# Stick-breaking attention in a fused decoder: one strict order for vector and scalar work, and weights split at fixed places of a turn

## The chip, the cores and the metric

The kernel runs on one core of a Trainium2 chip. Four engines matter here, and each takes its instructions in its own queue: TensorE (PE, matmuls; the loading of its stationary operand is listed as PEld), VectorE (DVE), ScalarE (ACT) and GpSimd (POOL). SyncE (SP) issues the transfers from memory. The metric is the device time of one execution, in microseconds (us).

## The reference, cut to what matters

A decoder trunk of two layers over 512 tokens of width 2048, in float32. The first layer is sparse attention; the second is stick-breaking attention with 16 query heads in four groups over four shared key/value heads, and a gate. The change touches the second layer only:

```python
q, gate = jnp.split(x @ w_in, [WIDTH_B], axis=-1)
z = jnp.einsum('bqngd,bsnd->bngqs', qg, k) * (HEAD_DIM ** -0.5)
log_om = jnp.where(strict, -jax.nn.softplus(z), 0.0)
suffix = lax.cumsum(log_om, axis=log_om.ndim - 1, reverse=True) - log_om
a = jnp.where(strict, jnp.exp(jax.nn.log_sigmoid(z) + suffix), 0.0)
o = jnp.einsum('bngqs,bsnd->bqngd', a, v)
return (o * jax.nn.silu(gate)) @ w_o
```

A token sees strictly earlier keys only; its weight for a key is a sigmoid times the product of what all keys between have left over, computed in log space.

## The kernel before

**Precision.** Each float32 product is made of three matmuls: every operand is split into a high part (a rounding copy on ScalarE) and a low part (a subtraction on VectorE), by `split` (line 131), and `mm3` (line 135) adds high by high, high by low and low by high in one PSUM bank.

**Two streams on TensorE.** TensorE's order is written out by hand. In the stage around the change it alternates between the gate projection and the attention of one group of four heads. The gate of a group is 64 *steps*: 16 blocks of weights by four banks, a step being one `mm3` into one bank (`gemm_w`, line 289; for group 0 `gate_first`, line 1214, which takes the blocks 8 to 15 first). A block of weights comes from the generator `items`: `next_raw` (line 179) issues its transfer, `split` makes the tiles wh and wl, of which there are three each.

**The attention** of a group (`Sticks`, line 1240) has ten units, pairs of a block of 128 queries and a block of 128 keys. The units with equal block numbers (0, 1, 5 and 8) lie on the diagonal and are masked. A unit passes through these methods:

- `logits`: three matmuls into a bank z; on the diagonal VectorE adds the mask. Unit 0 uses bank 7, the others banks 4 and 5 in turn.
- `soft` (abs, exp and ln on ScalarE) and `plus` (VectorE) make the softplus sp.
- `high` adds what earlier keys left (total) and makes sh on VectorE, and copies rows of z to t on ScalarE; `low` makes sl.
- `weights`: two matmuls with a triangular matrix add the running sum to z; ScalarE takes the exponential; VectorE subtracts z from t.
- `halves` splits the result a into high (ScalarE) and low (VectorE); `values`: three matmuls; `leave` copies a finished output.

`turn(s)` (line 1346) runs unit s's logits to `low`, unit s-1's `weights` and `halves`, and unit s-2's `values`, with gate steps in three gaps between.

**What sets the order on VectorE and ScalarE.** A planner orders what the program emits by a model of the time. Operations under `paced` (line 325) are recorded with `keep_in_program_order`; all others, the splits of the gate's weights above all, stand where the planner puts them. In the built program even paced operations of different kinds pass each other in places. Other splits lie in the deque `bg`: the next group's queries (`split_scaled`, line 1208), keys (`split_keys`) and the restoring of half of x's tiles (`restore`, line 1148). `pumped` (line 339) runs one of them every so many gate steps.

**Between groups** (lines 1398 to 1422) the two first logits of the next group come first, then four SiLUs of the gate's banks with a product each, then a table load for exp and ln (`log_exp`, line 1223), then `begin` for units 0 and 1. The SiLU's own table load is inserted by the compiler ahead of the first SiLU.

Of the kernel before, what the change touches and what calls it, by code (L numbers as in the profile page):

```python
# [77 lines left out]
def trunk_kernel(  # L78
# [17 lines left out]
    pe = nc.tensor  # L96
    pinned = [False]

    class Paced:


        def __init__(self, engine):
            self.engine_ = engine

        def __getattr__(self, name):
            method = getattr(self.engine_, name)
            if not callable(method):
                return method

            def call(*args, **kw):  # L110
                ins = method(*args, **kw)  # L111
# [96 lines left out]
    class Ahead:  # L208
# [13 lines left out]
        def __next__(self):  # L222
            self.prime()
            it = next(self.items, None)
            if it is not None:
                self.waiting.append(it)
            return self.waiting.popleft()

    def weight_parts():
        return tuple(top.tile([128, 512], F32R, name=n, tag=n, bufs=3) for n in ("wh", "wl"))  # L230

# [91 lines left out]
    bg = deque()  # L323

    def paced(fn, *args):
        was, pinned[0] = pinned[0], True
        fn(*args)
        pinned[0] = was

    def one():  # L330
        paced(bg.popleft())
# [270 lines left out]
    items = Ahead(all_items(), 2)  # L602
# [16 lines left out]
    late = slice(NSEL, T)  # L619
# [84 lines left out]
    banks = late_banks(range(4))  # L704
    gemm = gemm_w(items, late_plain, banks)
# [32 lines left out]
    banks = [bank(b, "v") for b in (4, 5, 6, 7)]  # L738
# [130 lines left out]
    for g in range(4):  # L869
        banks = mm_banks("g")  # L870
# [293 lines left out]
    def split_keys(g):  # L1164
        split(*K[g], Kf[:, g])
# [42 lines left out]
    def split_scaled(g, i):  # L1208
        qh, ql = (q.rearrange("p (h q) -> p h q", h=4) for q in Q[i])
        src = F[g][:, :, i * 128 : (i + 1) * 128]  # L1210
        act.activation(qh, src, AF.Copy, scale=HSCALE)
        dve.scalar_tensor_tensor(ql, src, HSCALE, qh.bitcast(F32), ALU.mult, ALU.subtract)

    def gate_first(banks):

        for kb in (*range(8, NK), *range(8)):
            wh, wl = next(items)
            for j, out in enumerate(banks):
                s = slice(j * 128, (j + 1) * 128)
                mm3(out, (wh[:, s], wl[:, s]), plain(kb), kb == 8, kb == 7)  # L1220
                yield

    def log_exp():
        tc.keep_in_program_order(act.preload_act_table_set("natural_log_exp_and_others"))

    def work():
        return px.tile([128, 512], F32, name="wk", tag="wk", bufs=6)

# [11 lines left out]
    class Sticks:  # L1240
# [101 lines left out]
        def begin(self, u):  # L1342
            for fn in (self.soft, self.plus, self.high, self.low):
                paced(fn, u)

        def turn(self, s, gemm, gaps):

            late = self.diagonal(s)
            if 1 < s < 10:
                paced(self.logits, s)  # L1350
                if late:
                    paced(self.low, s - 1)
                paced(self.soft, s)
                if not late:
                    paced(self.plus, s)
            steps(gemm, gaps[0])
            if s > 1:
                paced(self.values, s - 2)
            steps(gemm, gaps[1])
            if s < 11:  # L1360
                paced(self.weights, s - 1)
                if 1 < s < 10 and late:
                    paced(self.plus, s)
                paced(self.halves, s - 1)
                if 1 < s < 10:
                    paced(self.high, s)
                    if not self.diagonal(s + 1):
                        paced(self.low, s)
# [7 lines left out]
    QUERIES_DONE = {8: (1,), 9: (3,), 11: (0,)}, {5: (1,), 9: (3,), 11: (0,)}  # L1376

    log_exp()

    def after_combining(fn, *args):  # L1380
        with tc.issue_after(combined):
            fn(*args)

    bg.extend(lambda i=i: after_combining(split_scaled, 0, i) for i in (3, 1))
    banks = mm_banks("g")
    chunk = gate_first(banks)
    gemm = pumped(chunk)
    sticks = Sticks(0)
    for u, n in enumerate((9, 1)):
        steps(gemm, n)  # L1390
        paced(sticks.logits, u)
    for u in range(2):
        sticks.begin(u)
    bg.extend(lambda i=i: split_scaled(0, i) for i in (2, 0))
    steps(gemm, 8)
    gemm = pumped(chunk, 2)

    for g in range(4):
        if g:
            steps(gemm, 12)  # L1400
            bg.append(lambda g=g: split_scaled(g, 2))
        if 0 < g < 3:
            bg.append(lambda g=g: split_keys(g + 1))
        for s in range(1, 12):
            sticks.turn(s, gemm, (0 if s == 1 else 1, 1 if s > 1 else 0, 2 if s == 10 or not g and s % 2 else 3))
        run(gemm)
        drain()
        if g < 3:
            then = Sticks(g + 1)
            for u in range(2):  # L1410
                paced(then.logits, u)
        for h in range(4):
            sg = work()
            act.activation(sg, banks[h], AF.Silu)
            dve.tensor_tensor(F[g][:, h], F[g][:, h], sg, ALU.mult)
        if g < 3:
            sticks = then
            log_exp()
            for u in range(2):
                sticks.begin(u)  # L1420
# [60 lines left out]
```

## Time and profile before

| what | us |
|---|---|
| median of 3 runs (1878.97 to 1879.47) | 1879.23 |
| the profiled execution's own time | 1879.65 |
| its span, first to last instruction | 1877.9 |
| busy TensorE, VectorE, ScalarE | 1860.1, 1233.5, 938.0 |
| stick-breaking stage, from its first gate step to the first matmul of the output projection | 1233.96 to 1501.62 |

The profiled execution is the source of every duration below. In rows of the timeline the columns are the start in us from the start of the span, the length in us, engine, line, operation, output, inputs in the program's names, shapes, and in brackets the idle time before it with what ended it. `L111` is the helper that records every VectorE and ScalarE operation. Names: g are the gate's banks, z the logits, wh and wl the weight tiles, wk work tiles of the softplus and the weights, sh and sl its halves, c the tiles of keys, queries, values and of a, o the attention's output, f the stream. In rows by stretch the columns stand in the order PE, PEld, DVE, ACT, POOL (busy us, number of instructions), granted clock, DMA share, GB/s.

### The profile page before, as it was taken

The page shows a single profiled execution, that of the slowest core. Times are in us where ns is not written, and L with a number is a line of the kernel's source. Part 1 is how long each engine was busy: PE and PEld are TensorE (multiplying, and loading weights), DVE is VectorE, ACT ScalarE, POOL GpSimd, SP SyncE. Part 2 cuts the span into 40 slices and gives each one's busy share as a digit, 9 for nine tenths or more (in the row PEclk, how much of TensorE's full clock was granted, in tenths as well). Part 3 has the DMA queues.
Part 4 walks back from the last instruction along what each step waited for, and adds up shares of the span by engine and source line. Part 5 has one row for each costly group of instructions (what it writes and reads, how often), then busy time and mean ns, then how long its engine had stood idle before and what let it go on. Part 6 is the DMA issues. An engine that isn't in the chain of part 4 may idle for free.

```text
span 1877.9 us, 24827 instructions
## 1 busy us (share of the span) xinstructions
PE 1860.1 (99%) x9181; PEld 1573.8 (84%) x9181; DVE 1233.5 (66%) x2395; ACT 938.0 (50%) x1696; POOL 4.7 (0%) x20
## 2 busy tenths in 40 slices
PE   9999999999999999999999999999999999999998
PEld 8898888888888888888888999987777788888887
DVE  5668678566555455675367788887877745567534
ACT  3546333456554432474245444467778743347422
POOL 0000000000000000000000000000000000000000
PEclk9999999999999999999999999999999999999999
DMA  6442333322222532433343333322122253242333
GB/s 196 127 124 58 100 95 97 100 58 68 68 68 68 171 107 77 123 96 112 118 134 119 102 102 102 110 83 78 56 68 67 67 180 101 73 129 91 123 101 113
DMA packets 111178, 189.21 MB, mean 101 GB/s; under 512 B 8528, under 2 KB 29008, under 8 KB 111056
## 3 DMA queue, kind: packets, MB, share of 16 engines
q1 hardware_dynamic: 111056, 187.62, 32.5%
q8 instruction: 72, 1.18, 0.3%
q14 instruction: 50, 0.41, 0.1%
HBM read 179.21 MB, written 8.39 MB: 100 GB/s over the span
## 4 chain that ended last, share of the span: by engine, by line
PE 96%; DVE 2%; ACT 1%; issue 0%; DMA 0%; SPq 0%; DVEq 0%
PE g L136 12%; PE g L137 12%; PE g L138 12%; PE o L138 7%; PE o L137 7%; PE o L136 7%; PE m L136 4%; PE m L138 4%; PE m L137 4%; PE q L136 3%; PE q L138 3%; PE q L137 3%; PE k L137 2%; PE k L138 2%; PE k L136 2%; PE iq L138 1%
## 5 line engine op out<-in xcount | busy, mean ns | idle before, releaser
L111 ACT ACTIVATE wh<-raw 128x512 fp32r<-128x512 f32 (+3 forms) x685 | 397.7, 581 | 696.1 <-PE g L137 227.9
L111 DVE TENSOR_TENSOR wl<-raw,wh 128x512 fp32r<-128x512 f32 (+3 forms) x685 | 430.6, 629 | 453.3 <-ACT wh L111 434.7
L136 PE MATMUL g<-xh,wh 128*128 128x512 f32 x1024 | 403.9, 394 | 0.0
L138 PE MATMUL g<-xh,wl 128*128 128x512 f32 x1024 | 399.6, 390 | 0.0
L137 PE MATMUL g<-xl,wh 128*128 128x512 f32 x1024 | 399.5, 390 | 0.0
L138 PEld LDWEIGHTS g<-xh,wl 128*128 128x128 f32 x1024 | 192.2, 188 | 41.3
L137 PEld LDWEIGHTS g<-xl,wh 128*128 128x128 f32 x1024 | 192.5, 188 | 37.1
L136 PEld LDWEIGHTS g<-xh,wh 128*128 128x128 f32 x1024 | 192.4, 188 | 36.9 <-issue 0.3
L138 PE MATMUL o<-xh,wl 128*128 128x512 f32 x512 | 199.3, 389 | 0.0
L136 PE MATMUL o<-xh,wh 128*128 128x512 f32 x512 | 199.2, 389 | 0.0
L137 PE MATMUL o<-xl,wh 128*128 128x512 f32 x512 | 199.2, 389 | 0.0
L138 PEld LDWEIGHTS o<-xh,wl 128*128 128x128 f32 x512 | 96.1, 188 | 20.3 <-DVE wl L111 0.4
L137 PEld LDWEIGHTS o<-xl,wh 128*128 128x128 f32 x512 | 96.1, 188 | 20.1
L136 PEld LDWEIGHTS o<-xh,wh 128*128 128x128 f32 x512 | 96.1, 188 | 19.9
L136 PE MATMUL q<-xh,wh 128*128 128x512 f32 x256 | 99.6, 389 | 0.0
L137 PE MATMUL q<-xl,wh 128*128 128x512 f32 x256 | 99.6, 389 | 0.0
L138 PE MATMUL q<-xh,wl 128*128 128x512 f32 x256 | 99.6, 389 | 0.0
L111 ACT ACTIVATE sh<-st 128x512 fp32r<-128x512 f32 x80 | 49.7, 624 | 44.2 <-DVE st L111 44.2
L111 ACT ACTIVATE wk<-z 128x512 f32<-128x512 f32 x80 | 47.4, 593 | 43.1 <-PE z L1310 21.0
L111 DVE TENSOR_TENSOR sl<-st,sh 128x512 fp32r<-128x512 f32 x80 | 55.2, 690 | 13.9 <-ACT sh L111 13.9
L111 DVE TENSOR_TENSOR xl<-f,xh 128x512 fp32r<-128x512 f32 x80 | 54.3, 686 | 12.6 <-ACT f L111 12.3
L138 PEld LDWEIGHTS q<-xh,wl 128*128 128x128 f32 x256 | 48.0, 188 | 10.1
(287 smaller groups left out, 3319.0 us busy)
## 6 DMA issues: line engine op xcount, KB each, us to landing
raw<-w_in_a SPq DMA_DIRECT2D x95, 512.0 KB, 3.7
raw<-w_in_b SPq DMA_DIRECT2D x64, 512.0 KB, 3.7
raw<-w_ple_gate SPq DMA_DIRECT2D x52, 512.0 KB, 3.7
raw<-w_o_a SPq DMA_DIRECT2D x24, 512.0 KB, 3.7
raw<-w_o_b SPq DMA_DIRECT2D x24, 512.0 KB, 3.7
raw<-w_kv_b SPq DMA_DIRECT2D x16, 512.0 KB, 3.8
raw<-w_ple_gate SPq DMA_DIRECT2D x24, 256.0 KB, 2.9
f<-xT SPq DMA_DIRECT2D x4, 1024.0 KB, 6.3
```

What stands on the lines that cost most here:

```text
L111: ins = method(*args, **kw)
L136: pe.matmul(out, a[0], b[0], start=start, stop=False)
L137: pe.matmul(out, a[0], b[1], start=False, stop=False)
L138: pe.matmul(out, a[1], b[0], start=False, stop=stop)
```

## The change

All VectorE and ScalarE work of the stage is put in one order. A third state of the recorder (`pinned[0] == 2`, set by the new `strictly`) places each operation behind the one recorded before it on the same engine. The weight splits are under it too: `Fed` wraps `items` so that `push` emits the next block's splits and `next` only hands out what is there; `feed` pushes blocks until those that the next ten gate steps need are there. It is called inside a turn behind `plus` (one block at most, not in turns that begin on a diagonal unit), near the turn's end, and around the groups' starts. The splits in `bg` run at the ends of turns (`others`), one a turn, two in group 0. The SiLU table is loaded in turn 11 ahead of the last `leave`. The gate steps have new shares (`TURNS`): 17 instead of 18 ahead of group 0's first turn, 10 instead of 12 ahead of those of the later groups, a second step ahead of `values` in turns 5 and 8. `log_exp`, `begin`, `pumped` and `drain` are no longer used in this stage.

```diff
             def call(*args, **kw):
-                ins = method(*args, **kw)
-                if pinned[0]:
-                    tc.keep_in_program_order(ins)
+                if pinned[0] == 2 and self in newest:
+                    with tc.issue_after(newest[self].ins):
+                        ins = method(*args, **kw)
+                else:
+                    ins = method(*args, **kw)
+                    if pinned[0]:
+                        tc.keep_in_program_order(ins)
+                if pinned[0] == 2:
+                    newest[self] = ins
                 return ins
...
+        def push(self):
+            it = next(self.items, None)
+            if it is not None:
+                self.count += 1
+                self.waiting.append(it)
...
-        def turn(self, s, gemm, gaps):
+        def turn(self, s, gaps):
             late = self.diagonal(s)
-            if 1 < s < 10:
-                paced(self.logits, s)
+            new = 1 < s < 10
+            if new:
+                strictly(self.logits, s)
                 if late:
-                    paced(self.low, s - 1)
-                paced(self.soft, s)
+                    strictly(self.low, s - 1)
+                strictly(self.soft, s)
                 if not late:
-                    paced(self.plus, s)
-            steps(gemm, gaps[0])
+                    strictly(self.plus, s)
+                    feed(1)
+            gate(gaps[0])
             if s > 1:
-                paced(self.values, s - 2)
-            steps(gemm, gaps[1])
+                strictly(self.values, s - 2)
+            gate(gaps[1])
...
+            else:
+                strictly(act.preload_act_table_set, "silu_and_others")
             if s > 1:
-                paced(self.leave, s - 2)
-            steps(gemm, gaps[2])
+                strictly(self.leave, s - 2)
             if self.g < 3:
-                bg.extend(lambda i=i: split_scaled(self.g + 1, i) for i in QUERIES_DONE[self.g > 0].get(s, ()))
+                bg.extend(lambda i=i: split_scaled(self.g + 1, i) for i in {8 if self.g == 0 else 6: (1,), 9: (3,), 10: (0,)}.get(s, ()))
+            feed()
+            others(1 if self.g else 2)
+            gate(gaps[2])
...
+    def feed(most=9, ahead=10):
+        while most and items.count < min(64, -(-(gated[0] + ahead) // 4)):
+            strictly(items.push)
+            most -= 1
...
+    TURNS = (
+        ((0, 0, 2), (1, 1, 3), (1, 1, 2), (1, 1, 2), (2, 1, 2), (1, 1, 2), (1, 1, 3), (2, 1, 2), (1, 1, 2), (1, 1, 2), (1, 1, 3)),
+        ((0, 0, 3), *[(1, 1, 3)] * 3, (2, 1, 3), *[(1, 1, 3)] * 2, (2, 1, 3), (1, 1, 3), (1, 1, 2), (1, 1, 4)),
+    )
...
-            steps(gemm, 12)
-            bg.append(lambda g=g: split_scaled(g, 2))
...
+            if g and s == 2:
+                bg.append(lambda g=g: split_scaled(g, 2))
+            if 0 < g < 3 and s == 3:
+                bg.append(lambda g=g: split_keys(g + 1))
+            sticks.turn(s, TURNS[g > 0][s - 1])
...
         if g < 3:
             sticks = then
-            log_exp()
+            feed(1)
+            strictly(act.preload_act_table_set, LOG_EXP)
             for u in range(2):
-                sticks.begin(u)
+                for fn in (sticks.soft, sticks.plus, sticks.high, sticks.low):
+                    strictly(fn, u)
+                feed(1)
             banks = mm_banks("g")
-            gemm = pumped(gemm_w(items, plain, banks))
+            gemm = gemm_w(items, plain, banks)
+            for _ in range(5):
+                gate(2)
+                feed()
```

More of the change, by code (lines that the diff above doesn't have):

```diff
@@ L97, in trunk_kernel @@
     pinned = [False]
+    newest = {}
     class Paced:
@@ L227, in __next__, with __init__ @@
             return self.waiting.popleft()
+    class Fed:
+        def __init__(self, ahead):
+            self.items, self.waiting = ahead.items, ahead.waiting
+            self.count = len(self.waiting)
+        def push(self):
[3 more added lines that the diff above has]
+                self.waiting.append(it)
+        def __next__(self):
+            return self.waiting.popleft()
     def weight_parts():
@@ L326, in paced, with strictly @@
         was, pinned[0] = pinned[0], True
+        fn(*args)
+        pinned[0] = was
+    def strictly(fn, *args):
+        was, pinned[0] = pinned[0], 2
         fn(*args)
@@ L1354, in turn @@
                 if not late:
-                    paced(self.plus, s)
-            steps(gemm, gaps[0])
+                    strictly(self.plus, s)
+                    feed(1)
+            gate(gaps[0])
             if s > 1:
-                paced(self.values, s - 2)
-            steps(gemm, gaps[1])
+                strictly(self.values, s - 2)
+            gate(gaps[1])
             if s < 11:
[L1361 to L1366, printed above, removed]
+                strictly(self.weights, s - 1)
+                if new and late:
+                    strictly(self.plus, s)
+                strictly(self.halves, s - 1)
+                if new:
+                    strictly(self.high, s)
@@ L1410, in trunk_kernel, with close @@
             for u in range(2):
-                paced(then.logits, u)
-        for h in range(4):
+                strictly(then.logits, u)
+        def close(h):
             sg = work()
@@ L1415, in trunk_kernel @@
             dve.tensor_tensor(F[g][:, h], F[g][:, h], sg, ALU.mult)
+        for h in range(4):
+            strictly(close, h)
         if g < 3:
             sticks = then
-            log_exp()
+            feed(1)
+            strictly(act.preload_act_table_set, LOG_EXP)
             for u in range(2):
-                sticks.begin(u)
+                for fn in (sticks.soft, sticks.plus, sticks.high, sticks.low):
+                    strictly(fn, u)
+                feed(1)
             banks = mm_banks("g")
-            gemm = pumped(gemm_w(items, plain, banks))
+            gemm = gemm_w(items, plain, banks)
+            for _ in range(5):
+                gate(2)
+                feed()
     pk_.close()
```

45 lines of the change are left out of this document (25 added, 20 removed).

## The prediction

> **What bounds the kernel now.** I read the page first, then the busy time of each engine by stretch, then the waits inside the stick-breaking stage, then its timeline.
>
> ```profile
> span 1877.9 us, 24827 instructions
> PE 1860.1 (99%) x9181; PEld 1573.8 (84%) x9181; DVE 1233.5 (66%) x2395; ACT 938.0 (50%) x1696; POOL 4.7 (0%) x20
> PE 96%; DVE 2%; ACT 1%; issue 0%; DMA 0%; SPq 0%; DVEq 0%
> ...
> raw<-w_in_b SPq DMA_DIRECT2D x64, 512.0 KB, 3.7
> ```
>
> TensorE ends the chain, so only its pauses can change. The next fence gives the four groups of the stage, cut at the first logits matmul of the next group. Each row holds the length, then PE, PEld, DVE, ACT and POOL busy time, clock, DMA share and GB/s.
>
> ```profile
> 1233.96:1305.04 71.08, 65.03 (x274) 50.09 (x273) 55.45 (x95) 52.10 (x94) 1.24 (x6) 1.00 0.25 76
> 1305.04:1370.93 65.89, 63.98 (x274) 50.54 (x273) 51.09 (x82) 51.08 (x88) 0.00 (x0) 1.00 0.22 65
> 1370.93:1436.95 66.02, 64.01 (x273) 50.38 (x272) 50.50 (x81) 51.09 (x88) 0.00 (x0) 1.00 0.21 65
> 1436.95:1501.62 64.67, 63.34 (x274) 50.38 (x272) 48.94 (x79) 50.79 (x87) 0.00 (x0) 1.00 0.22 66
> ```
>
> A group is 64 gate steps of three matmuls (192) and ten units of eight (80): 272 matmuls. Unhindered ones start 0.227 us apart (next fence, 1323.04 to 1323.27 and on to 1323.49), so a group needs 61.7 us. Lost are 9.4, 4.2, 4.3 and 3.0 us: 20.9 in all, 1.1% of the span. That is the most the change can win. VectorE and ScalarE work about 51 us of each 61.7: what costs is when an operation comes, not how much there is.
>
> ```profile
> 1256.60 0.50 PE L136 MATMUL z<-c,c 128*128 128x512 f32 x1 [1.60 <-DVE t L111]
> 1273.81 0.50 PE L136 MATMUL z<-c,c 128*128 128x512 f32 x1 [1.31 <-DVE t L111]
> ...
> 1319.95 0.50 PE L1334 MATMUL o<-c,c 128*128 128x512 f32 x1 [0.79 <-DVE c L111]
> 1323.04 0.39 PE L137 MATMUL g<-xl,wh 128*128 128x512 f32 x1
> 1323.27 0.39 PE L138 MATMUL g<-xh,wl 128*128 128x512 f32 x1
> 1323.49 0.39 PE L136 MATMUL z<-c 128*128 128x512 f32 x1
> ...
> 1339.72 0.50 PE L136 MATMUL z<-c 128*128 128x512 f32 x1 [0.31 <-DVE t L111]
> ```
>
> Logits of unit u wait for the subtraction t of unit u-2, which still reads their bank; the third value matmul waits for the low half c. Each pause costs about 0.16 more than its wait.
>
> **A turn in rows.** One turn of group 1, from its logits, with the steps between left out:
>
> ```profile
> 1324.37 0.60 ACT L111 ACTIVATE wk<-z 128x512 f32<-128x512 f32 x1 [0.27 <-PE z L138]
> 1325.00 1.30 ACT L111 ACTIVATE wk<-wk 128x512 f32<-128x512 f32 x2
> 1326.21 0.39 PE L1310 MATMUL z<-sh,tri 128*128 128x512 f32 x1
> 1326.33 0.69 DVE L111 SCALAR_TENSOR_TENSOR wk<-z,wk 128x512 f32<-128x512 f32 x1
> 1326.88 0.60 ACT L111 ACTIVATE wk<-z 128x512 f32<-128x512 f32 x1 [0.57 <-PE z L1310]
> 1327.51 0.67 DVE L111 TENSOR_TENSOR t<-t,z 1x512 f32<-1x512 f32 x1 [0.48 <-ACT wk L111]
> 1328.17 0.69 DVE L111 TENSOR_TENSOR c<-wk,c 128x512 fp32r<-128x512 f32 x1
> 1328.90 0.75 DVE L111 SCALAR_TENSOR_TENSOR wk<-t,ident,wk 32x512 f32<-32x512 f32 x1
> ...
> 1371.47 1.90 DVE L111 TENSOR_TENSOR f<-f,wk 128x512 f32<-128x512 f32 x3 [1.22 <-ACT wk L111]
> ```
>
> So: abs 0.88 after the first logits matmul, plus 1.96 after abs, exp 0.67 after the first weights matmul, t 0.63 after exp. VectorE starts 0.60 to 0.66 apart (three in 1.90), ScalarE about 0.55 to 0.63.
>
> **The change, part by part.** The built program has the same instructions: 9183 matmuls and the like on TensorE, 1634 on ScalarE with equally many table loads, 2335 on VectorE, and the DMA queue's list is unchanged. Gate shares, the order on VectorE and ScalarE, and so the pauses, move. I walk the new order with the durations above.
>
> *An ordinary turn of 23 matmuls (5.21 us).* From its logits: ln ends at 2.8, the weight copy now fixed behind it ends at 3.4, just when exp may start (2.72 + 0.67). VectorE: plus 2.84, wl 3.45, t 4.1, done 4.75. The next logits come at 5.21: no pause, 0.45 us to spare. With 20 matmuls (4.53) it pauses 0.2 to 0.3. The turns that begin on a diagonal unit get a second step ahead of the values; in groups 1 to 3 their t is done 0.4 to 0.5 before TensorE asks. That removes the pauses at 1339.72 (0.31 + 0.16), the like ones behind it and the one at 1319.95 (0.79 + 0.16) from groups 1 to 3.
>
> *Start of a group.* The old order let exp of unit 0 and weight copies pass the chain of unit 1 (next fence: 1248.52 lies ahead of 1250.31). The strict one does not.
>
> ```profile
> 1242.07 0.60 ACT L111 ACTIVATE wk<-z 128x512 f32<-128x512 f32 x1 [1.82 <-DVE z L111]
> ...
> 1245.69 0.59 ACT L111 ACTIVATE t<-z 32x512 f32<-32x512 f32 x1 [0.84 <-DVE wk L111]
> 1246.31 0.60 ACT L111 ACTIVATE wk<-z 128x512 f32<-128x512 f32 x1
> ...
> 1248.52 0.58 ACT L111 ACTIVATE wk<-z 128x512 f32<-128x512 f32 x1
> ...
> 1250.31 0.59 ACT L111 ACTIVATE t<-z 32x512 f32<-32x512 f32 x1
> ...
> 1302.61 1.28 ACT L111 ACT_TABLE_LOAD   x1
> 1303.90 0.60 ACT L111 ACTIVATE wk<-g 128x512 f32<-128x512 f32 x1
> ...
> 1307.51 1.28 ACT L111 ACT_TABLE_LOAD   x1
> 1308.80 0.60 ACT L111 ACTIVATE wk<-z 128x512 f32<-128x512 f32 x1
> ```
>
> Groups 1 to 3, counted from the new group's first logits: ScalarE reaches the SiLUs at 0.05 (from exp of unit 9 at -5.2: seven operations of about 0.57 and a load of 1.3), four of them 2.1, a weight copy 0.6, a load 1.3, abs 0 at 4.05. Plus 0 at 6.0, t copy 6.7, abs 1 at 7.3, plus 1 at 9.25, t copy 9.95, and only then the copy of the group's fourth weight block: 10.55, its low half ready at 11.9. TensorE wants that low half in the 13th step, at 10.43 (logits 1.36, ten steps 6.8, weights 0.45, two steps and two matmuls 1.82). New pause: 1.55 with the refill. Behind that copy on ScalarE stand the fifth block's, exp 0 and the high half that the first values read; they are done at 12.9, the values come at 13.6, so nothing is added. In group 3 two splits of the output stage (0.6 each on ScalarE) stand between: 2.4.
>
> *The SiLU table ahead.* Both orders load twice per boundary, in 1.28 with the next operation 0.01 behind; the load now lies a leave and a weight copy earlier, under gate steps. On its own: nothing, under the cover of the four steps behind the last values (2.7); without it, 1.3 a boundary.
>
> The Trainium skill ("ScalarE: Activation LUTs", What ACT_TABLE_LOAD costs) adds a drain of about 1.38 us to the 1.283 us of a load. The two loads above show the 1.28 and no drain; by the Trainium skill's figure the sum would be 8.3 us longer (six loads), an estimate.
>
> *Start of group 0.* Abs 0 stays at 1242.07. Plus 0 1244.03, t copy 1244.7, abs 1 1245.3, plus 1 1247.3, t copy 1248.0, then copies of two weight blocks and two query splits (2.2): exp 0 at 1250.75 instead of 1248.52, the low half done at 1253.0. TensorE wants it at 1250.7: 2.35 lost.
>
> *Turns of group 0.* Two kinds of work are now fixed at the ends of turns:
>
> ```profile
> L111 ACT ACTIVATE c<-f 128x512 fp32r<-128x512 f32 x16 | 9.7, 619 | 0.0
> L111 DVE TENSOR_TENSOR xl<-raw,xh 128x256 fp32r<-128x256 f32 x8 | 3.3, 417 | 0.8 <-ACT xh L111 0.8
> L111 ACT ACTIVATE xh<-raw 128x256 fp32r<-128x256 f32 x8 | 3.2, 403 | 0.0
> ```
>
> Behind the diagonal turn 5 ScalarE has t copy, leave, two weight copies and two restores (2.9 in all) before abs 6, which so comes at 3.4 of turn 6 instead of 0.88; plus 6 and exp 5 follow at 5.35, t of unit 5 at 6.0, done at 6.6. The logits of turn 7 want it at 4.53: 2.2 lost with the refill. In groups 1 to 3, without restores and with a longer turn, it is 0.45. Logits 6 and 9 lose 1.1 each, because restores or key splits stand before the diagonal mask on VectorE. Low halves in turns 5, 8 and 10 and logits 4 come to 1.9. With 2.35 that is 8.65, against 9.4.
>
> *What costs nothing, and its cover.* Weight blocks are asked for nine steps ahead (6 us with the attention between); a copy waits at most for the one step that frees its buffer, and what it then holds up, the next abs, waits for later logits anyhow. Without that cover a late block costs its delay, as in the fourth block above. The transfer of x holds its buffer until two turns' restores are done; the w_in_b transfer queued behind it lands 3.7 us later, about 1.7 before its copy; past that it would cost one for one. POOL's list is unchanged.
>
> **Sum.** Group 0 8.65; groups 1 and 2 1.55 + 0.45 + 0.4 of uneven intervals (of the old 4.2 as much is in none of the pauses above 0.05) = 2.4 each; group 3 2.4 + 0.45 + 0.35 = 3.2. Total 16.7 against 20.9: 4.2 gained. The profiled execution took 1879.65, the median is 1879.23: 1875.4 and 1875.0. **Forecast 1875.0**, just beyond the 0.2% (3.8 us) that a measurement of this kernel can tell from no change. Bounds of the unknown: at best every boundary pause and half of group 0's goes (1.55 + 1.55 + 2.4 + 3 = 8.5 more, 1866.5); at worst the turns lengthen as in the third rival.
>
> **Rivals.**
>
> *Faster, 1869.5 (1866 to 1872).* The boundary copy is not late: ScalarE catches up while the SiLUs wait for their banks. 1.55 + 1.55 + 2.4 = 5.5 less. For: the old ScalarE shows abs 0 at 1308.80, 3.76 after the logits at 1305.04, with fewer operations fixed ahead. Against: two chains of 1.96 + 0.7 + 0.6 can't be shortened.
>
> *No change, 1879.5 (1877 to 1882).* The wl now fixed ahead of t makes t late: 0.45 is all there is to spare, and three sites a group (logits 3, 4, 7) would pay 0.31 + 0.16: 12 x 0.47 = 5.6 back, less one paid already. It decides from 0.45 of delay on.
>
> *Slower, 1884.5 (1883 to 1888).* VectorE becomes the bound of turns. Plus, wl, t, low half, total, high and low take 4.3 of 5.21 us; where a query split (0.6) or two restores (0.8) go with it, 4.9 to 5.1, and in a strict order any wait for ScalarE above 0.1 to 0.3 adds to the turn. About 20 such turns at 0.47: 9.4 more. For: 13 waits of VectorE's t for ScalarE. Against: group 0's VectorE busy 55.45 of 71.08.
>
> ```profile
> DVE t L111 <- ACT wk L111: 12.9, 13, 1.4
> PE z L136 <- DVE t L111: 5.5, 8, 1.6
> PE o L1334 <- DVE c L111: 2.4, 3, 0.8
> ```
>
> *A load that drains, 1882.7.* A load fixed between two operations could hold the next one as long again as it lasts: six times 1.28 on the path of the fourth block, 7.7. Against it: the operations behind 1302.61 and 1307.51 start 0.01 after the load's end. The Trainium skill's rule on the drain ("ScalarE: Activation LUTs", What ACT_TABLE_LOAD costs) is of this kind.
>
> **How the numbers follow.** Forecast 0.42 (own range 1872 to 1878), faster rival 0.24, no change 0.12, slower 0.20, drain 0.02. Against the median, faster by over 0.2% is below 1875.5: the faster rival and, as the forecast lies at that edge but most of its errors shorten it (I added every hand-over in full), 0.28 of its 0.42, so 0.52. Slower is above 1883: 0.20. The rest is 0.28. The range 1867 to 1884 leaves out the upper part of the slower rival and the lower edge of the faster.
>
> **What would show it.** Right: in groups 1 and 2 no pause before logits 3 and 4, one of 1 to 2 us before the gate matmul on the fourth weight block (wh or wl the releaser), one of 0.3 before logits 7; in group 0 about 2.3 before the first values and 2 before logits 7; groups of 70.3, 64.1, 64.1 and 64.9 us. Wrong: group lengths near 62 (faster), pauses before logits in most turns with wl or another split just ahead on VectorE (no change, slower), ScalarE gaps behind table loads (drain).

## The result, and the profile after

The changed kernel takes **1874.94 us** (median of 12 runs, 1873.81 to 1876.13) against 1879.40 for the kernel before: a ratio of 0.9976, 95% interval 0.9967 to 0.9985. The profiled execution took 1875.82, 3.8 less than that of before. Its page (span, busy time, the chain that ended last):

```profile
span 1874.1 us, 24812 instructions
PE 1857.8 (99%) x9181; PEld 1576.2 (84%) x9181; DVE 1232.3 (66%) x2395; ACT 939.8 (50%) x1696; POOL 4.7 (0%) x20
PE 93%; ACT 3%; DVE 2%; issue 1%; DMA 0%; SPq 0%; DVEq 0%; ACTq 0%
```

The work is the same, only TensorE's pauses differ. The four groups by stretch, cut as before (length; busy PE, PEld, DVE, ACT, POOL; clock; DMA share; GB/s):

```profile
1233.90:1305.66 71.76, 66.14 (x275) 51.45 (x273) 55.30 (x95) 52.55 (x94) 1.23 (x6) 0.98 0.25 74
1305.66:1369.28 63.62, 62.61 (x274) 50.69 (x272) 50.00 (x82) 51.62 (x88) 0.00 (x0) 1.00 0.22 67
1369.28:1432.88 63.60, 62.59 (x274) 50.70 (x272) 50.01 (x82) 51.63 (x88) 0.00 (x0) 1.00 0.22 67
1432.88:1497.78 64.90, 62.93 (x274) 50.65 (x272) 50.14 (x81) 51.81 (x88) 0.00 (x0) 1.00 0.21 65
```

Against 71.08, 65.89, 66.02 and 64.67 before: groups 1 and 2 gain 2.3 and 2.4, group 3 is as long as it was, and group 0 is 0.7 longer, at a mean clock of 0.98. What is left in groups 1 to 3 lies at their starts. The timeline of group 1's, ScalarE and the one pause of TensorE:

```profile
1308.08 1.28 ACT L116 ACT_TABLE_LOAD   x1
1309.37 0.60 ACT L116 ACTIVATE wk<-z 128x512 f32<-128x512 f32 x1
...
1315.36 0.59 ACT L116 ACTIVATE t<-z 32x512 f32<-32x512 f32 x1 [0.76 <-DVE wk L116]
1315.98 1.15 ACT L116 ACTIVATE wh<-raw 128x512 fp32r<-128x512 f32 x2
1316.66 0.50 PE L145 MATMUL g<-xh,wh 128*128 128x512 f32 x1 [0.87 <-ACT wh L116]
```

The fourth block's copy (1315.98) stands behind the t copy of unit 1, and the gate waits for it. Losses are counted from the matmuls' starts, as what the intervals have over the cadence of 0.227. The intervals around this pause lose 1.41; in group 2 it is 1.42, in group 3, where two splits of the output stage stand between, 2.4 behind a wait of 1.83 (below, in the fence of `end_of_turn_only`). Logits 7 lose 0.41 (at 1344.85), logits 3 and 4 nothing. Group 0's pauses:

```profile
1251.23 0.63 ACT L116 ACTIVATE c<-wk 128x512 fp32r<-128x512 f32 x1
1251.92 0.50 PE L1359 MATMUL o<-c,c 128*128 128x512 f32 x1 [1.75 <-ACT c L116]
1253.05 0.50 PE L1361 MATMUL o<-c,c 128*128 128x512 f32 x1 [0.41 <-DVE c L116]
...
1274.03 0.50 PE L145 MATMUL z<-c,c 128*128 128x512 f32 x1 [0.70 <-DVE t L116]
1280.61 0.50 PE L145 MATMUL z<-c,c 128*128 128x512 f32 x1 [1.75 <-DVE t L116]
1292.20 0.50 PE L145 MATMUL z<-c,c 128*128 128x512 f32 x1 [0.70 <-DVE t L116]
```

The first row is the high half that the first values (1251.92, 1253.05) wait for; below are logits 6, 7 and 9. Behind the first values something came that no row of before had shown (by stretch, columns as above):

```profile
1252.00:1254.00 2.00, 1.59 (x6) 1.03 (x7) 1.26 (x3) 1.94 (x4) 0.00 (x0) 0.98 0.40 156
1254.00:1255.00 1.00, 1.00 (x4) 0.78 (x3) 1.00 (x2) 0.19 (x1) 0.00 (x0) 0.50 0.00 0
1255.00:1256.00 1.00, 1.00 (x4) 0.74 (x3) 0.07 (x1) 0.66 (x2) 0.00 (x0) 0.50 0.00 0
1256.00:1257.00 1.00, 1.00 (x4) 0.80 (x3) 0.97 (x2) 1.00 (x2) 0.00 (x0) 0.50 0.74 185
1257.00:1258.00 1.00, 1.00 (x5) 0.77 (x5) 0.97 (x2) 0.04 (x1) 0.00 (x0) 0.83 0.97 339
```

For 3.4 us the granted clock is 0.50, and matmuls run 0.43 us apart. The 12 runs fall into six of 1873.8 to 1874.6 (mean granted clock of the whole run 0.999 to 1.000) and six of 1875.2 to 1876.1 (0.998 to 0.999); the profiled one is of the upper six.

### The profile page after: what moved, and what is told of

It reads as the page before. It is cut to its first block, busy times and chain, and to the rows that moved or that the text cites. A ratio compares the mean times of both kernels' runs of the same rounds, so it can differ in the third digit from the quotient of the medians.

```text
span 1874.1 us, 24812 instructions
## 1 busy us (share of the span) xinstructions
PE 1857.8 (99%) x9181; PEld 1576.2 (84%) x9181; DVE 1232.3 (66%) x2395; ACT 939.8 (50%) x1696; POOL 4.7 (0%) x20
## 4 chain that ended last, share of the span: by engine, by line
PE 93%; ACT 3%; DVE 2%; issue 1%; DMA 0%; SPq 0%; DVEq 0%; ACTq 0%
PE g L145 11%; PE g L147 11%; PE g L146 11%; PE o L145 7%; PE o L147 7%; PE o L146 7%; PE m L145 4%; PE m L147 4%; PE m L146 4%; PE q L145 3%; PE q L147 3%; PE q L146 3%; ACT wk L116 2%; PE k L147 2%; PE k L146 2%; PE k L145 2%
## 5 line engine op out<-in xcount | busy, mean ns | idle before, releaser
L118 ACT ACTIVATE wh<-raw 128x512 fp32r<-128x512 f32 (+2 forms) x624 | 359.5, 577 | 688.4 <-PE g L146 220.4
L118 DVE TENSOR_TENSOR wl<-raw,wh 128x512 fp32r<-128x512 f32 (+2 forms) x624 | 388.2, 623 | 439.6 <-ACT wh L118 424.9
```

## The experiments

All medians below stand beside runs of the kernel before on the same chip (1879.35 to 1879.66).

**Is it the strictness?** The new positions and shares, but the planner's order:

```diff
 def strictly(fn, *args):
-    was, pinned[0] = pinned[0], 2
+    was, pinned[0] = pinned[0], True
```

> The changed positions of the weights, of the SiLU table and the changed gate shares stay, but the order on each engine is the planner's again, as in the kernel before. Theory (the gain comes from the strict order, which keeps both places of the weights in a turn where they are written): the pauses of the kernel before, before logits 3, 4 and the values, come back in the turns, and the time is within 1 us of the kernel before, 1878.5 to 1879.8. Rival (the gain comes from the gate shares and the places, whatever orders the instructions): the time is 1873.5 to 1875.8, like the changed kernel. Second rival: the strict order costs at the starts more than it gives in the turns; then this is faster than the changed kernel, 1871 to 1873.

Measured 1875.19 (1873.96 to 1876.26; ratio 0.9976, 0.9966 to 0.9987). The theory fell. The built program has the very same sequence of operations on VectorE and ScalarE: once every operation, the weight splits among them, is recorded at a fixed place, the planner's order is the written one. Strictness adds nothing; the places and shares are the change. These eight runs are therefore eight more of the changed kernel, in the same two clusters.

**The shares without the places.** The kernel before with the new shares alone (`steps(gemm, 7)` and `10`, and `TURNS`):

> The kernel before with the changed gate shares and nothing else: two steps ahead of turn 1 of group 0 fewer by one, ten instead of twelve ahead of the turns of groups 1 to 3, a second step ahead of the values in the turns that begin on a diagonal unit. Order and places of weights, splits and tables are those of the kernel before. So far the changed order with the old shares took 1879.68 us, as long as the kernel before, and the changed shares with one place of the weights 1879.50. Theory (shares and places work only together: the shares give the diagonal turns their second step, the places keep the weight copies from running into the chains): the pauses before logits 3, 4 and 7 of groups 1 to 3 change sites but not their sum of about 4 us a group, and the time is 1878 to 1881. Rival (the shares alone give the gain, and the places only keep it): groups 1 to 3 lose 1.5 to 2.5 us each, the time is 1873 to 1876.

Measured 1876.63 (1876.38 to 1876.78; ratio 0.9985, 0.9977 to 0.9994): 2.8 us of the 4.5, so my theory fell and the rival was 0.6 too low (of its 1.5 to 2.5 lost a group, groups 1 and 2 lose 3.5 and only group 3 keeps within it, 2.0). Its group 1 by stretch:

```profile
1304.41:1369.62 65.21, 63.02 (x273) 50.74 (x272) 50.12 (x81) 51.15 (x88) 0.00 (x0) 1.00 0.21 65
```

and that group's pauses in the timeline:

```profile
1321.80 0.50 PE L136 MATMUL z<-c 128*128 128x512 f32 x1 [1.25 <-DVE t L111]
1344.19 0.50 PE L136 MATMUL z<-c 128*128 128x512 f32 x1 [0.51 <-DVE t L111]
...
1363.80 0.50 PE L1310 MATMUL z<-sl,tri 128*128 128x512 f32 x1 [0.22 <-DVE sl L111]
```

Logits 3 wait 1.25, logits 7 0.51, the second matmul of unit 9's weights 0.22. The places remove the first and the last, halve the second, and bring the fourth block's pause: 65.2 becomes 63.6.

**The places without the shares.**

```diff
-    for n in (3, 2, 2):
+    for n in (3, 2, 3):
...
-            for _ in range(5):
+            for _ in range(6):
```

and `TURNS` of 1, 1, 3 in turns 2 to 9 (1, 1, 2 in group 0's odd ones and in turn 10).

> The changed order and the changed places of the weights with the gate shares of the kernel before: three steps ahead of turn 1 in group 0's last share instead of two, six pairs behind the start of groups 1 to 3 instead of five, one step ahead of the values also in the turns that begin on a diagonal unit. Theory (the second step ahead of the values in diagonal turns gives the subtraction t its time): logits 3, 4 and 7 of groups 1 to 3 and logits 6 and 9 of group 0 pause 0.2 to 0.5 us longer each, some 2 to 4 us in all, while the extra step at the starts covers 0.45 of the pause before values 0 of group 0 and, in groups 1 to 3, comes too late for the fourth block: the time is 1876 to 1878.5. Rival (the shares do nothing, the places of the weights did it): 1873.5 to 1875.5. Second rival (all of the gain is in the shares, and the order costs as much as it gives): 1879 to 1880.

Measured 1879.68 (1877.85 to 1881.4; ratio 1.000, 0.9991 to 1.0009): the second rival's time, but not its cause. Group 1, group 3 and one us behind group 3's start by stretch:

```profile
1304.86:1369.97 65.11, 63.29 (x273) 50.70 (x273) 50.03 (x81) 52.09 (x89) 0.00 (x0) 1.00 0.21 65
1434.59:1501.72 67.13, 64.44 (x273) 51.81 (x272) 50.26 (x81) 51.77 (x88) 0.00 (x0) 0.97 0.20 63
...
1448.00:1449.00 1.00, 1.00 (x4) 0.81 (x3) 0.97 (x3) 0.97 (x2) 0.00 (x0) 0.50 0.47 37
```

The pauses of both starts and of logits 7 in its timeline:

```profile
1316.40 0.50 PE L145 MATMUL g<-xh,wh 128*128 128x512 f32 x1 [1.27 <-ACT wh L116]
1346.19 0.50 PE L145 MATMUL z<-c 128*128 128x512 f32 x1 [0.53 <-DVE t L116]
1446.84 0.80 PE L145 MATMUL g<-xh,wh 128*128 128x512 f32 x1 [2.12 <-ACT wh L116]
```

Group 1 gains 0.8 by the places, but with the old shares the fourth block is wanted earlier (1.27 for 0.87) and logits 7 too; in group 3 the pause of 2.12 is followed by half the clock, and 67.1 against 64.7 eats most of what groups 0 to 2 gained. Over the four groups the trace is 0.4 shorter than before, and would be about 2.0 shorter without the 1.6 that the halved clock costs (worked out for group 0 in the section on the prediction). The one run whose mean clock is recorded as 1.000 took 1877.85, 1.8 less than before. So the places alone do gain, and in most runs the clock takes it away.

**The second place in a turn.** Without `feed(1)` behind `plus`:

> The changed kernel without the weight block that is fed behind the sum of a turn's unit: all blocks of a turn are fed at its end, so that on VectorE the low half of a block no longer stands between that sum and the subtraction t, and in every fourth turn or so two blocks stand in a row at the end. Theory (t is done 0.45 us before TensorE asks, so the 0.6 us of the low half ahead of it cost nothing but in the short turns): the pauses of 0.30 before logits 7 go and those of group 0 shrink by up to 0.6 each, two low halves in a row give back as much before the next turn's sum, and the time is 1873 to 1875.5. Rival (the early place is what removed the pauses before logits 3 and 4): six pauses of 0.3 to 0.5 come back in groups 1 to 3 and the time is 1877 to 1878.5. Second rival (the low half ahead of t is what costs in all turns): 1871 to 1872.5.

Measured 1879.50 (1877.21 to 1880.38; ratio 0.9997, 0.9988 to 1.0006). The median is beyond all three, but the 11 runs stand on three levels: three at 1877.2 to 1877.6 (mean clock 0.999 to 1.000), three at 1878.8 to 1879.5 (0.998 to 0.999, the profiled one among them) and five at 1879.9 to 1880.4 (0.998). The lowest lies in the first rival's range. Groups 1 and 3 and one us behind group 3's start by stretch:

```profile
1305.05:1369.32 64.27, 62.93 (x274) 50.60 (x272) 50.08 (x82) 51.54 (x88) 0.00 (x0) 1.00 0.21 66
1433.65:1500.78 67.13, 64.78 (x274) 51.72 (x272) 50.11 (x81) 51.77 (x88) 0.00 (x0) 0.97 0.20 63
...
1448.00:1449.00 1.00, 1.00 (x4) 0.74 (x3) 0.61 (x1) 0.67 (x2) 0.00 (x0) 0.50 0.80 281
```

and in the timeline logits 7 of group 1 and the fourth block's wait in group 3, then the latter in the changed kernel:

```profile
1344.86 0.50 PE L145 MATMUL z<-c 128*128 128x512 f32 x1 [0.37 <-DVE t L116]
1445.89 0.50 PE L145 MATMUL g<-xh,wh 128*128 128x512 f32 x1 [1.84 <-ACT wh L116]
```

```profile
1445.12 0.50 PE L145 MATMUL g<-xh,wh 128*128 128x512 f32 x1 [1.83 <-ACT wh L116]
```

Groups 1 and 2 are 0.7 longer: logits 4 lose 0.38 and logits 7 0.64, against nothing and 0.41. Ahead of logits 4 two low halves in a row at a turn's end hold up the next sum; at logits 7 two stand in a row in both kernels, and what adds 0.23 there isn't shown. So the first rival was right in kind, for logits 4 and 7 in place of 3 and 4. The early place is worth about 0.7 a group, group 0 and group 3 included, though it puts a low half ahead of t. Of the 2.2 us that group 3 is longer in the profiled execution the other 1.6 are the clock, halved behind a wait of 1.84. Why it is halved here and not in the changed kernel's profile, with a wait of 1.83 at the same place, stays open. Behind the first values of group 0 it is the other way round: they wait 1.76 and 0.40 here too, and this profile has full clock behind them.

**The SiLU table ahead.** Without the `preload_act_table_set` of turn 11:

> The changed kernel without the SiLU table asked for at the end of turn 11: the table is loaded when the first SiLU comes, one leave and one weight copy later on ScalarE. Theory (ScalarE reaches the SiLUs with the same sum of work, and abs 0 of the next group behind them): 1.28 us lie at another place of ScalarE's row, the pauses before the 13th gate step stay at 1.0 to 1.1 and 2.0 us, and the time is within 0.3 us of the changed kernel with its two clusters, 1873.8 to 1876.1. Rival (asked for early, the load lies under gate steps that ScalarE would otherwise idle through): each boundary is 0.6 to 1.3 us longer, 1876.5 to 1878.5 in all. Second rival (a load behind other work holds the next operation): the next operation starts 1 us or more behind the load's end and the boundary is that much longer.

Measured 1873.56 (1873.36 to 1874.86; ratio 0.9969, 0.9956 to 0.9982): no dearer, as I had it; the median is 0.2 below my theory's range. The fourth block's wait is 0.96 for 0.87, so the early load gives 0.1 a boundary; in group 3 the planner also puts the two output splits, which are not under `strictly`, two operations later, and the wait there is 1.29 for 1.83. The table's effect can't be told from that. This run's profile has the same two pauses at the start of group 0 as the changed kernel (timeline), and no drop of the clock behind them (by stretch):

```profile
1252.21 0.50 PE L1359 MATMUL o<-c,c 128*128 128x512 f32 x1 [1.76 <-ACT c L116]
1253.35 0.51 PE L1361 MATMUL o<-c,c 128*128 128x512 f32 x1 [0.41 <-DVE c L116]
```

```profile
1254.00:1255.00 1.00, 1.00 (x6) 0.82 (x5) 1.00 (x2) 0.49 (x1) 0.00 (x0) 1.00 0.00 0
```

**What makes a start late.** First less work there: `others(1)` dropped from the loop ahead of group 0's first turn, so that two query splits come later.

> Group 0's start without its two query splits (each a copy on ScalarE and a subtraction on VectorE): they come behind turn 1 instead. Nothing else is changed. Theory (the pause before values 0 at 1251.92, 1.75 us, and the one before the low half at 1253.05, 0.41 us, come from exp 0 standing behind unit 1's chain and the two splits; and the stretch from 1254 to 1257 at a granted clock of 0.50 comes from those pauses): values 0 lose about 1.1 us less (0.6 to 0.9 are left), no matmul runs at 0.43 us a step, and the time is 1.1 to 1.3 us under the faster half of the changed kernel's runs, about 1872.7, without a second cluster at 1875.6. Rival (the two splits are done before exp 0 is wanted; unit 1's chain alone makes it late): the pause stays at 1.75 us and the time at 1873.9 or 1875.6. Second rival (the low clock there has nothing to do with the pauses): the pause shrinks, and stretches at 0.50 are still seen at 1254 to 1257.

Measured 1873.66 (1873.25 to 1874.88; ratio 0.9971, 0.9959 to 0.9982). The first values wait 0.71 instead of 1.75, as expected; logits 3 then wait 0.22, and 0.7 is gained. Four runs lie at 1873.3 to 1873.8 and two at 1874.7 and 1874.9: the upper cluster is still there, against the theory, and the time is 1.0 above it. No clock below 1 stands at this place in the one profile, which is of the lower four. Where it drops in the other two isn't known; the start of group 3 is possible, whose wait of 1.83 is unchanged, since two other traces show the drop there (`old_shares` behind 2.12, `end_of_turn_only` behind 1.84).

Then the fourth block ahead of unit 1's chain:

```diff
             for u in range(2):
                 for fn in (sticks.soft, sticks.plus, sticks.high, sticks.low):
                     strictly(fn, u)
                 feed(1)
+                for _ in range(2 + u):
+                    gate(2)
+                    feed()
...
-            for _ in range(5):
-                gate(2)
-                feed()
```

> At the starts of groups 1 to 3, unit 0's chain is issued, then two pairs of gate steps with their feeds, then unit 1's chain, then the other three pairs: the copy and the subtraction of the fourth weight block stand between the two units' chains. Group 0's start is as in the changed kernel. Theory (ScalarE takes its work in the order given, and at a start there is more of it than TensorE's filling covers): the pause of 1.0 to 1.4 us before the 13th gate step (2.0 and more in group 3) goes, but exp 0 stays behind unit 1's chain and the fourth copy is now ahead of it too, so values 0 lose about 1.1 us of their own: a gain of 0.2 to 0.4 us a start, 0.6 to 1.2 in all, the time at about 1873.0 (1874.7 where the low clock of group 0 strikes). Rival (the copy of the fourth block alone is late, exp 0 has slack): 1.2, 1.2 and 2.2 us are gained, together 4.6, the time at about 1869.3.

Measured 1875.90 (1873.84 to 1877.4; ratio 0.9981, 0.9972 to 0.999): as the theory has it in kind, without its small gain: the four groups of the profiled execution are together 0.1 longer than the changed kernel's, both with one halving of the clock. The median is higher because only two of the 11 runs are below 1874.3 and three stand at 1877.0 to 1877.4 (mean clock 0.998); no trace shows where those three lose it. The block's copy is early, and the values wait in its place (timeline of group 1):

```profile
1316.06 0.63 ACT L116 ACTIVATE wh<-raw 128x512 fp32r<-128x512 f32 x1
1316.72 0.60 ACT L116 ACTIVATE wk<-z 128x512 f32<-128x512 f32 x1
1317.35 0.63 ACT L116 ACTIVATE c<-wk 128x512 fp32r<-128x512 f32 x1
...
1318.03 0.50 PE L1359 MATMUL o<-c,c 128*128 128x512 f32 x1 [0.80 <-ACT c L116]
1318.92 0.50 PE L1361 MATMUL o<-c,c 128*128 128x512 f32 x1 [0.16 <-DVE c L116]
```

Last, exp 0 too, ahead of what nobody waits for yet:

```diff
-            for u in range(2):
-                for fn in (sticks.soft, sticks.plus, sticks.high, sticks.low):
-                    strictly(fn, u)
-                feed(1)
...
-            for _ in range(5):
-                gate(2)
-                feed()
+            for fn in (sticks.soft, sticks.plus, sticks.high, sticks.low):
+                strictly(fn, 0)
+            for u in range(2):
+                for _ in range(2 + u):
+                    gate(2)
+                    feed()
+                if not u:
+                    strictly(sticks.soft, 1)
+                    strictly(sticks.plus, 1)
...
                 strictly(self.halves, s - 1)
+                if s == 1:
+                    strictly(self.high, 1)
+                    strictly(self.low, 1)
```

and the like in group 0, with its query splits later.

> At all four starts unit 0's chain is issued whole, then two pairs of gate steps with their feeds, then unit 1's absolute value, exponential, logarithm and its sum, then exp 0 and the halves of the weights; unit 1's rounding to its high half and its low half come behind those of exp 0, in turn 1. Group 0's query splits come behind turn 1. Theory (what is late at a start is late by its place in ScalarE's and VectorE's order, not by the amount of work): the pauses before values 0 of group 0 (1.75 and 0.41 us), before the 13th step (0.87, 0.88, 1.83 us and the small ones after it) go, and with them the low clock at 1254: 2.2 + 1.4 + 1.4 + 2.4 = 7.4 us under the slower runs less 1.6 for the clock, the time at about 1867 to 1868. Rival (the work of a start fills the engines: whichever piece goes last is late): unit 1's weights take the place, with a pause of 1 to 1.5 us before weights 1 at each start, and the time is 1872 to 1874.

Measured **1869.18** (1868.5 to 1869.72; ratio 0.9945, 0.9933 to 0.9958), better than both kernels, its five runs in one cluster. Groups 0 to 2 by stretch, and the pause that came instead in group 0's timeline (the first row is cut at 1233.90; this kernel's first gate step is at 1233.28, so that its group 0 takes 68.7):

```profile
1233.90:1302.00 68.10, 63.74 (x272) 49.79 (x271) 54.58 (x93) 51.80 (x94) 1.23 (x6) 1.00 0.23 77
1302.00:1364.42 62.42, 62.28 (x274) 50.76 (x273) 49.86 (x82) 51.40 (x88) 0.00 (x0) 1.00 0.21 68
1364.42:1426.78 62.36, 62.22 (x273) 50.71 (x272) 49.81 (x82) 51.35 (x88) 0.00 (x0) 1.00 0.22 68
```

```profile
1254.44 0.50 PE L145 MATMUL z<-c,c 128*128 128x512 f32 x1 [0.90 <-DVE t L116]
```

Groups 1 and 2 are within 0.7 of the 61.7 that their matmuls need. The time is 1.2 above the theory's upper end, because in group 0 the t of unit 1 is now late for logits 3 (0.90 and the refill), and in group 3 the values of unit 0 still lose 1.0.

**The restores behind turn 5.** On top of that order, `others(0)` instead of two in turn 5 of group 0:

> The order of starts of exp_first (which took 1869.18 us), and in group 0 the two restored blocks of x that stood at the end of turn 5 move one turn on. Theory (the pause before logits 7 of group 0, 1.9 us in every kernel with this order so far, comes from work on ScalarE behind the diagonal turn 5 that stands ahead of unit 6's absolute value): two restores are 1.3 us of ScalarE's time there, the pause falls by 0.7 to 1.3 us, nothing else moves, and the time is 1867.9 to 1868.5. Rival (TensorE's pauses only move: what is put off is late one turn on): the pause before logits 8 or 9 grows by as much, and the time stays at 1868.8 to 1869.7.

Measured 1869.26 (1869.09 to 1869.46; ratio 0.9945, 0.9932 to 0.9957): the rival. The timelines' rows of logits 7, of this kernel and then of `exp_first`:

```profile
1276.78 0.50 PE L145 MATMUL z<-c,c 128*128 128x512 f32 x1 [1.13 <-DVE t L116]
```

```profile
1276.97 0.50 PE L145 MATMUL z<-c,c 128*128 128x512 f32 x1 [1.76 <-DVE t L116]
```

The 0.63 gained there is lost again before the values of unit 8, where the trace has 0.5 in intervals too short for a wait of their own, and in group 0 as a whole nothing is left.

**The clock.** Three copies of a bank more on ScalarE lengthen the pause of the changed kernel; four bring a pause into the order of `exp_first`:

```diff
+            if not g and s == 1:
+                for _ in range(3):
+                    strictly(act.activation, work(), sticks.state[1][0], AF.Copy)
```

> The changed kernel with three copies of a bank more on ScalarE (their results are not used) between group 0's start and the exp of unit 0: about 1.8 us, so that the pause before values 0 is 3.5 us instead of 1.75 and the 0.41 before the low half stays. The changed kernel ran its next 3 us at a granted clock of 0.50 in about half of its executions (the two clusters, 1873.8 to 1874.6 and 1875.2 to 1876.1). Theory (how long TensorE pauses within some us decides whether the clock is halved behind it): with 3.5 us it is halved every time, all runs in one cluster at 1877.3 to 1878.0 (1.8 for the copies and 1.6 for the clock over the lower cluster). Rival (the drop is a matter of chance that has nothing to do with the length of the pause): two clusters again, 1875.6 to 1876.4 and 1877.0 to 1877.9.

> The kernel exp_first (1869.18 us, one cluster, no pause before values 0) with four such copies on ScalarE at the place where it hands the exp of unit 0 on: about 2.4 us, so that a pause of 1.8 to 2.4 us comes back before values 0. Theory (the pause itself brings the two clusters, whatever the order that made it): the time is 1871.0 to 1871.7 in some runs and 1.4 to 1.8 us more in others. Rival (the clusters come with the changed kernel's order of the weight copies at the starts, not with the pause): one cluster, 1871.0 to 1871.7.

The longer pause: 1876.93 (1876.55 to 1877.8, 11 runs; ratio 0.9988, 0.9979 to 0.9997). The wait is 3.22 and the one at the low half is down to 0.06, so the pauses grow by 1.1, less than I had counted, and eight of the runs lie below the theory's 1877.3. The lower cluster would then stand near 1875.1 (1874.0, the median of the changed kernel's six faster runs, and 1.1), where there is no run. Eight lie where the halved clock puts them (1875.2 to 1876.1, and 1.1), and three, at 1877.6 to 1877.8, higher still; no trace shows why. The pause in the timeline, and the us behind it by stretch:

```profile
1253.49 0.50 PE L1359 MATMUL o<-c,c 128*128 128x512 f32 x1 [3.22 <-ACT c L116]
```

```profile
1254.00:1255.00 1.00, 0.94 (x3) 0.63 (x3) 0.22 (x1) 0.97 (x2) 0.00 (x0) 0.72 0.00 0
1255.00:1256.00 1.00, 1.00 (x3) 0.74 (x3) 0.72 (x2) 0.77 (x2) 0.00 (x0) 0.50 0.00 0
1256.00:1257.00 1.00, 1.00 (x4) 0.77 (x3) 0.57 (x1) 0.00 (x0) 0.00 (x0) 0.50 0.00 0
1257.00:1258.00 1.00, 1.00 (x4) 0.79 (x3) 0.25 (x1) 0.84 (x2) 0.00 (x0) 0.58 0.18 50
```

`exp_first_late`: 1871.37 (1870.78 to 1872.84; ratio 0.9959, 0.9947 to 0.9972), three runs of 1870.8 to 1871.4 and two of 1872.5 and 1872.8, where the order alone had one cluster. The waits were two, and not one of 2 (timeline):

```profile
1250.87 0.50 PE L1359 MATMUL o<-c,c 128*128 128x512 f32 x1 [1.03 <-ACT c L116]
1256.67 0.50 PE L145 MATMUL z<-c,c 128*128 128x512 f32 x1 [1.31 <-DVE t L116]
```

Both runs speak for pauses, and not the order, as what brings the clusters; the profile of the second is one at full clock, so the place of its drops isn't shown.

## Why the prediction was right, and where only in sum

Forecast 1875.0, measured 1874.94. That they agree so closely is luck: the median falls into the gap between the six faster and the six slower runs, where no run lies. Against the faster ones (median 1874.0) the forecast is 1.0 too long, mostly in one term, the uneven intervals; the other half of the runs lose 1.6 by a term that was not there at all. Groups forecast at 70.3, 64.1, 64.1, 64.9 measured 71.8, 63.6, 63.6, 64.9.

- **The start of groups 1 to 3.** Right in place, cause and nearly in size: the copy of the fourth block behind both chains, 1.41, 1.42 and 2.4 lost there against 1.55, 1.55 and 2.4. The wait ends on the block's high half (wh, 0.87); the low half, for which the sum was made, adds only 0.16 two matmuls later. The parts held too: abs 0 came 3.71 after the group's first logits (forecast 4.05), the copy 10.32 (10.55), and the next operation 0.01 behind the table load. The drain was not seen there either, so the rival that stood on it did not happen.
- **Why the copy stands there.** Wrong in words: I put it down to the strict order. `paced_only` builds the same sequence without it; recording the splits at fixed places is enough.
- **Ordinary turns.** Right: logits 3 and 4 of groups 1 to 3 lose nothing, logits 7 0.41 (forecast 0.45). The 0.4 of uneven intervals was too much: less than 0.1 is left in groups 1 and 2. With the 0.14 of the start that makes them 0.5 shorter than forecast. The price of a pause was too small: it costs 0.27 more than its wait, 0.16 in its own interval and 0.11 in the next (1.75 became 2.03 at logits 7 of group 0), not 0.16.
- **The place ahead of t.** The forecast let it cost nothing, and it does: logits 3 and 4 of groups 1 to 3 wait for no t. That it gains was not foreseen; without it each group is about 0.7 longer.
- **Group 0.** Its pauses were forecast at 8.65. The intervals of the changed kernel lose 10.1, of which 1.6 is the halved clock (4.33 around the first values, against 2.75 in `no_preload` with the same pauses): 8.5. Single terms were off both ways: the first values 2.75 for 2.35, logits 7 2.0 for 2.2, logits 6 and 9 1.0 each for 1.1, the rest 1.7 for 1.9.
- **The term that was missing** is the clock: 1.6 us in about half of the runs, behind a pause that I had foreseen. Without it the kernel takes 1874.0, 5.4 less than before, not the 4.2 of the sum.
- **The rivals.** The time of the faster one, 1869.5, was there to be had, but not by ScalarE catching up: `exp_first` had to move exp 0 and the fourth block ahead of unit 1. Late t in most turns (no change) and VectorE as the bound (slower) did not show: no pause in those turns, and VectorE busy 50.0 of 63.6. The sum of the no-change rival does not come out as written: 5.6 less one site of 0.47, added to 1875.0, is 1880.1, not 1879.5.

What each part gave: the shares alone 2.8, the places alone nothing in the median, both 4.5. Where the clock stays whole it is 2.8, 1.8 to 2.0 and 5.4, so there the parts nearly add up. What hides the gain of the places is the clock: with the old shares the fourth block is wanted earlier, and the longer pause in group 3 halves it.

## What to carry to other kernels

When work that the scheduler used to place freely is given fixed places, look first at where chains begin: in the steady turns there was slack to hide it, at the group starts the piece written last was late, whichever it was, until the one that TensorE asks for first was also written first. Test a place and a share together and apart, and look at single runs as well as the median: here the median showed nothing of what the places alone gave. And add up the pauses of a dense TensorE stream that lie within a few us, not only each by itself: a pause can cost more than its length.

## What the runs showed of the hardware

Behind some of the longer pauses the granted clock fell to 0.50, for the same time in both traces whose rows stand above in full. The sum of the missing clock over the rows, divided by 0.5, is 3.4 us in the changed kernel (0.02 x 2, three times 0.50, 0.17) and in `longer_pause` (0.28, 0.50, 0.50, 0.42). At half the rate that is 1.7 us of work; the intervals show 1.6 (4.33 against 2.75). It is a matter of chance with waits of 1.75 and 0.41 a us apart (11 of the 20 runs are in the upper cluster, and `no_preload` has the same waits at full clock); by the times, it came in all 11 runs with 3.22. Which runs had the drop is read from their times and mean clocks; the place is seen only in the profiled ones. The ten runs of `exp_first` and `both`, whose longest waits were 1.76 and 1.13 with nothing near them, show one cluster, and so do the 11 of `shares_alone`, whose longest in this stage was 1.27.

The Trainium skill ("TensorE: Matmul & The Clock Gate", Part 1: The HAM clock gate) has the clock decided over free-running windows of 3.4 us and halved after one idle window. The length of the slow stretch agrees (3.4), and windows that start at any time could explain the chance, which no run here shows; but here waits of 1.84, or of 1.75 and 0.41, were enough, with matmuls before, between and behind, so in this kernel less than a whole idle window does it. How much less, these runs don't tell.
